# First layer's first gate vector summed on VectorE, with a chunk-by-chunk norm and a small-block scan

## The chip, the cores and the metric

One core of a Trainium2 chip runs the whole program. Its engines are named as in the profile: PE (TensorE matmuls) and PEld (its weight loads), DVE (VectorE), ACT (ScalarE), POOL (GpSimd) and SP (SyncE, which here only issues DMAs). The metric is the device time of one execution in microseconds, the median of several.

## The reference

Two layers of a hybrid network act on two groups of 128 tokens of width 2048: a prompt (group 0) and a sample (group 1). All is float32.

```
for l in 0, 1:
    shift1, scale1, gate1, shift2, scale2, gate2 = split(silu(c) @ w_mod[l] + b_mod[l], 6)   # one c a group
    h = x * (1 + scale1) + shift1
    q, k, v, hq, hff, hfb, hi, hgt = split(h @ w_in[l])            # 2048 -> 6656
    att = rms_norm(attention(q, k, v, sink))                       # 8 heads; sample also sees a cache
    hg  = rms_norm(scan_fwd + scan_bwd) * silu(hgt)                # 8 heads, chunks of 32 tokens
    x = layer_norm(ALPHA * x + gate1 * (concat(att, hg) @ w_o[l]))
    f = square(relu((x * (1 + scale2) + shift2) @ w_up[l])) @ w_down[l]   # 2048 -> 8192 -> 2048
    x = layer_norm(ALPHA * x + gate2 * f)
```

A scan, per head and chunk of 32 tokens: `o = tril(q e^b (k e^-b)^T) v + (q e^b) S` and `S = decay * S + (k e^(b_last - b))^T v`, with b the running sum of the log gates; the backward scan runs over the flipped tokens. The outputs are x of both groups, the prompt's k and v, and the prompt's final scan states.

## The kernel before

**Weights.** Every product with a weight matrix is done in tiles of 512 x 512. SP loads a tile as two halves of 128x1024 (`raw`, 10 buffers), ACT casts each half to fp32r (`wh`, line 1324) and DVE forms the rest (`wl = raw - wh`, line 1325); four `wh` and four `wl` buffers hold two tiles, and the split runs one tile ahead. The activations are split likewise, and PE adds three products, hi*hi, hi*lo, lo*hi (`mm_tile`, lines 436 to 450). A unit is the tiles that sum into one output, up to four of them (`groups`). Kind T (lines 436 to 439) leaves the output transposed, kind N (448 to 450) with tokens on partitions, one PSUM bank a token group. PSUM has three `acc` banks for the units, one for the modulation, four for the rest.

**Modulation.** A vector of 2048 of `c @ w_mod` reads 16 MB. `Mod` and `ModQ` multiply on PE with the two columns of c as weights (lines 203 and 223, four column groups at a time). `ModH` instead multiplies raw tiles by a scalar a partition and sums them in two accumulators on DVE (line 266; the first pass of a half on ACT, line 264), adds over the partitions with ones on PE (line 275) and stores a gate vector as a row in DRAM. `POOLED` lists the vectors done so; before, gate2 of layer 0 and shift1, scale1, gate1, gate2 of layer 1.

**Order.** `layer` writes one list `seq` of weight tiles, modulation items of 1 MB and calls. `RATE` says how many PE items follow a tile on the average, `PRATE` how many `ModH` items; `GAP` puts six PE items behind the first tile after a norm. Layer 0's in-projection runs over its 13 units three times (first 512 of the inputs, second, and the other half), since its modulation comes in quarters. Between tiles `pump` advances generators (attention, scans, norms) by a step each: up to two in the middle of a tile and up to three behind it, first come first. POOL and SP issue in the order of the program; the order on PE, DVE and ACT is chosen at compile time by the framework's scheduler. A tile name has a fixed number of buffers (`BUFS`: Y and Z 8, G, s0 and w 2).

**Scan** (`scan_task`). After the diagonal blocks (`pI`, line 748) the three later chunks get their products with all earlier ones, in three rounds, each with full 128-column weights (`pX`, line 777) and a scaling of the earlier keys before the next (line 774); a mask (`fx`, `bx`) copies the wanted blocks (line 794).

**Norm.** `ln_head` normalizes all eight pieces of 128x512 (line 909); then `ln_mod` goes chunk by chunk: transpose (931), scale and shift (group 0 on DVE in two passes, lines 934 and 936, group 1 on ACT, 940), split (408, 409). `ln_out` multiplies and adds the norm's own weights on POOL (1002, 1003) as soon as it is reached; after layer 0 its rows go to DRAM (1270).

Of the kernel before, what the change touches and what calls it, by code (L numbers as in the profile page):

```python
# [8 lines left out]
F32 = mybir.dt.float32  # L9
# [9 lines left out]
T = 128  # L19
# [42 lines left out]
def tile_hybrid_step(ctx: ExitStack, tc: tile.TileContext, a, o):  # L62
# [353 lines left out]
    def mm_tile(it, between):  # L416
# [6 lines left out]
        e = kg == un.groups[-1]  # L423
        for kk in range(2):
            if kk == 1:
                between()
            ks = range(2 * kk, 2 * kk + 2)
            if un.kind == "T":
                for m in range(4):
                    if f and kk == 0 and m % 2 == 0:  # L430
                        un.ps[m // 2] = accp.tile([128, 512], F32, tag="acc", name=nm("acc"))
                    ps = un.ps[m // 2][:, 256 * (m % 2):256 * (m % 2) + 256]
                    for k in ks:
                        w0 = wh[k][:, 128 * m:128 * m + 128]
                        w1 = wl[k][:, 128 * m:128 * m + 128]
                        pe.matmul(ps, lhsT=w0, rhs=hi[:, k], start=f and k == 0 and m % 2 == 0, stop=False,  # L436
                                  skip_group_check=True)
                        pe.matmul(ps, lhsT=w0, rhs=lo[:, k], start=False, stop=False, skip_group_check=True)  # L438
                        pe.matmul(ps, lhsT=w1, rhs=hi[:, k], start=False, stop=e and k == 3 and m % 2 == 1,  # L439
                                  skip_group_check=True)  # L440
            else:
                for g in range(2):
                    if f and kk == 0:
                        un.ps[g] = accp.tile([128, 512], F32, tag="acc", name=nm("acc"))
                    ps = un.ps[g]
                    gs = slice(128 * g, 128 * g + 128)
                    for k in ks:
                        pe.matmul(ps, lhsT=hi[:, k, gs], rhs=wh[k], start=f and k == 0, stop=False)  # L448
                        pe.matmul(ps, lhsT=hi[:, k, gs], rhs=wl[k], start=False, stop=False)  # L449
                        pe.matmul(ps, lhsT=lo[:, k, gs], rhs=wh[k], start=False, stop=e and k == 3)  # L450
# [233 lines left out]
    def scan_task(l, G, p, dr, z):  # L684
# [72 lines left out]
        mb = lambda s: masks[mk + s].unsqueeze(1).to_broadcast([128, 4, 128])  # L757
        dve.copy_predicated(v3(aT, 4), mb("i"), v3(pI, 4))
# [3 lines left out]
        order = [0, 1, 2, 3] if fwd else [3, 2, 1, 0]  # L762
        pX = bank("pX")
        qS = lf[:, 256:512]
        for i in range(1, 4):
            c = order[i]
            pc = order[:i]
            if i >= 2:
                sl = slice(min(pc[:-1]), max(pc[:-1]) + 1)
                n = i - 1  # L770
                d = dm[:, :, pc[-1]:pc[-1] + 1].unsqueeze(3).to_broadcast([128, 4, n, 32])
                kk = kdv[:, :, sl, :]
                flat = lambda x: x.rearrange("p m c t -> p m (c t)")
                dve.tensor_tensor(flat(kk), flat(kk),
                                  dm[:, :, pc[-1]:pc[-1] + 1].to_broadcast([128, 4, n * 32]), ALU.mult)
            for m in range(4):
                pe.matmul(pX[:, 128 * m + 32 * c:128 * m + 32 * c + 32], lhsT=kd[:, 128 * m:128 * m + 128],  # L777
                          rhs=qb[:, 128 * m + 32 * c:128 * m + 32 * c + 32], start=True, stop=True)
            if i == 1:
                cum = small(8).rearrange("p (h c) -> p h c", h=2)  # L780
                for hl in range(2):
                    m = 2 * hl + 1
                    dve.memset(cum[:, hl, order[0]:order[0] + 1], 1.0)
                    for x in range(1, 4):
                        pcol, ccol = order[x - 1], order[x]
                        dve.tensor_tensor(cum[:, hl, ccol:ccol + 1], cum[:, hl, pcol:pcol + 1],
                                          dm[:, m, pcol:pcol + 1], ALU.mult)
                for hl in range(2):
                    dve.tensor_tensor(
                        qS[:, 128 * hl:128 * hl + 128].rearrange("p (c t) -> p c t", c=4),  # L790
                        qbv[:, 2 * hl + 1], cum[:, hl, :].unsqueeze(2).to_broadcast([128, 4, 32]), ALU.mult)
            yield
        cs = slice(32 * min(order[1:]), 32 * max(order[1:]) + 32)
        dve.copy_predicated(v3(aT, 4)[:, :, cs],
                            masks[mk + "x"][:, cs].unsqueeze(1).to_broadcast([128, 4, 96]),
                            v3(pX, 4)[:, :, cs])
        pc = order[:3]
        lc = order[3]
        for m in (0, 2):
            sl = slice(128 * m + 32 * min(pc), 128 * m + 32 * max(pc) + 32)  # L800
            dve.tensor_scalar(kd[:, sl], kd[:, sl], dm[:, m, lc:lc + 1], None, ALU.mult)
# [67 lines left out]
    yt = {}  # L869
# [14 lines left out]
    def add_gated(key, n, g, ps, gt, first, last):  # L884
# [6 lines left out]
        else:  # L891
            (dve if n == 3 else pool).tensor_tensor(y, y, t, ALU.add)
# [10 lines left out]

    def ln_head(key):
        mr = ln_stat(key)
        for n in range(4):
            for g in range(2):
                y = yt[key, n, g]
                dve.tensor_scalar(y, y, mr[g][0], mr[g][1], ALU.subtract, ALU.mult)
# [11 lines left out]

    def ln_mod(key, AB, dst):

        A, B = AB
        for n in range(4):
            hl = new_act("h")
            for g in range(2):
# [5 lines left out]
                if g == 0:  # L933
                    dve.tensor_tensor(v3(t, 4), v3(pt, 4),
                                      A[:, 4 * n:4 * n + 4, g:g + 1].to_broadcast([128, 4, 128]), ALU.mult)
                    dve.tensor_tensor(v3(t, 4), v3(t, 4),
                                      B[:, 4 * n:4 * n + 4, g:g + 1].to_broadcast([128, 4, 128]), ALU.add)
                else:
                    for c in range(4):
                        act.activation(t[:, 128 * c:128 * c + 128], pt[:, 128 * c:128 * c + 128], AF.Identity,  # L940
                                       scale=A[:, 4 * n + c, g:g + 1], bias=B[:, 4 * n + c, g:g + 1])
# [51 lines left out]
    def ln_out(key, li, sink_fn):  # L993

        tag = "G"
# [488 lines left out]
```

## Time and profile before

| | |
|---|---|
| median of 3 runs | 2641.58 us (2641.39 to 2647.34) |
| profiled execution | 2641.68 us, span 2639.9 us |
| mean clock granted to TensorE | 0.988 |
| busy PE, PEld, DVE, ACT, POOL | 2536.6, 2178.1, 1862.5, 1214.5, 230.9 us |
| HBM | 643.32 MB read, 246 GB/s over the span |

Busy time is the union of an engine's instructions. A matmul's end is modelled, so PE counts as busy up to where the next one starts. The stages can be told by their lines: the first two rounds of layer 0 end near 122 and 222 us, its in-projection near 455, output projection near 608, MLP from 626 to 1391; then layer 1 with in-projection from 1409, output projection to 1880, MLP from 1898 to 2620, and the last norm.

### The profile page before, as it was taken

The numbers are of one execution on the slowest core, as the hardware profiler recorded it, in microseconds if no ns is written. First come the engines' busy times: TensorE is split into PE (matmuls) and PEld (weight loads), VectorE is DVE, ScalarE is ACT, GpSimd is POOL, SyncE is SP. The second block draws the span as 40 slices with busy tenths as digits, with TensorE's granted clock in tenths as the row PEclk, the third lists the DMA queues.
The fourth block names the chain that finished last, engine by engine and source line by source line (L and its number), as shares of the span: only waits on it lengthen the run. The fifth ranks groups of instructions, "written<-read, shape, count | busy, mean of one in ns | idle before, by whom it ended". The sixth has DMA issues, their size and how long they took to land.

```text
span 2639.9 us, 41114 instructions
## 1 busy us (share of the span) xinstructions
PE 2536.6 (96%) x16276; PEld 2178.1 (83%) x16276; DVE 1862.5 (71%) x2290; ACT 1214.5 (46%) x1655; POOL 230.9 (9%) x266
## 2 busy tenths in 40 slices
PE   7999999998999999999999999999799999999996
PEld 4787777756988979979887989888798998998985
DVE  3455777658887777887778888877865565656656
ACT  3434554434444533534434656644454454443442
POOL 2000000014100000000014100001420000000003
PEclk9999999999999999999999999999899999999998
DMA  9889778868887878787879556566566666666663
GB/s 359 287 283 324 265 244 273 297 231 323 281 307 276 276 261 287 265 281 258 287 251 331 195 191 204 177 228 212 186 225 208 222 202 227 212 207 225 205 206 115
DMA packets 192369, 652.91 MB, mean 247 GB/s; under 512 B 22752, under 2 KB 25376, under 8 KB 192176
## 3 DMA queue, kind: packets, MB, share of 16 engines
q1 hardware_dynamic: 177680, 614.56, 68.0%
q0 software_dynamic: 11552, 33.04, 4.4%
q8 instruction: 127, 2.08, 0.3%
q10 hardware_dynamic: 2944, 2.69, 0.3%
q14 instruction: 66, 0.54, 0.1%
HBM read 643.32 MB, written 6.88 MB: 246 GB/s over the span
## 4 chain that ended last, share of the span: by engine, by line
PE 76%; DMA 10%; DVE 9%; issue 3%; ACT 1%; SPq 0%; POOL 0%; DVEq 0%; ACTq 0%; POOLq 0%
PE acc L436 12%; PE acc L439 12%; PE acc L438 12%; PE acc L448 11%; PE acc L449 11%; PE acc L450 11%; DMA raw<-in_w_mod_dram 6%; DVE wl L1325 3%; DVE ma L266 2%; PE psm L203 2%; PE pX L777 1%; DMA raw<-in_w_up_dram 1%; DMA raw<-in_w_in_dram 1%; PE psm L223 1%; DMA out_nsf_dram<-lf 1%
## 5 line engine op out<-in xcount | busy, mean ns | idle before, releaser
L1324 ACT CAST wh<-raw 128x1024 fp32r<-128x1024 f32 x784 | 821.8, 1049 | 1140.3 <-PE acc L450 489.0
L1325 DVE TENSOR_TENSOR wl<-raw,wh 128x1024 fp32r<-128x1024 f32 x784 | 971.2, 1246 | 433.3 <-ACT wh L1324 406.6
L436 PE MATMUL acc<-hh,wh 128*128 128x256 f32 x3072 | 875.9, 285 | 3.4 <-DVE q L599 1.9
L439 PE MATMUL acc<-hh,wl 128*128 128x256 f32 x3072 | 870.5, 284 | 7.9 <-DVE wl L1325 7.7
L438 PE MATMUL acc<-hl,wh 128*128 128x256 f32 x3072 | 869.7, 283 | 1.2 <-DVE hl L409 1.2
L436 PEld LDWEIGHTS acc<-hh,wh 128*128 128x128 f32 x3072 | 589.0, 192 | 39.2 <-issue 26.0
L439 PEld LDWEIGHTS acc<-hh,wl 128*128 128x128 f32 x3072 | 588.6, 192 | 11.2 <-DVE wl L1325 10.4
L438 PEld LDWEIGHTS acc<-hl,wh 128*128 128x128 f32 x3072 | 589.0, 192 | 2.9 <-DVE hl L409 2.2
L266 DVE SCALAR_TENSOR_TENSOR ma<-raw,stat,ma 128x1024 f32<-128x1024 f32 x300 | 388.5, 1313 | 113.4 <-DMA raw<-in_w_mod_dram 111.8
L448 PE MATMUL acc<-wh,fh 128*128 128x512 f32 x1024 | 401.8, 392 | 7.0 <-DVE Z L1236 6.8
L449 PE MATMUL acc<-wl,fh 128*128 128x512 f32 x1024 | 400.4, 391 | 0.4 <-DVE wl L1325 0.4
L450 PE MATMUL acc<-wh,fl 128*128 128x512 f32 x1024 | 399.7, 390 | 0.0
L448 PEld LDWEIGHTS acc<-wh,fh 128*128 128x128 f32 x1024 | 193.0, 188 | 57.8 <-DVE Z L1236 8.1
L449 PEld LDWEIGHTS acc<-wl,fh 128*128 128x128 f32 x1024 | 193.0, 188 | 40.8 <-DVE wl L1325 1.5
L450 PEld LDWEIGHTS acc<-wh,fl 128*128 128x128 f32 x1024 | 193.1, 189 | 40.4
L448 PE MATMUL acc<-wh,hh 128*128 128x512 f32 x320 | 129.5, 406 | 3.0 <-ACT hh L408 2.4
L449 PE MATMUL acc<-wl,hh 128*128 128x512 f32 x320 | 127.5, 398 | 0.3 <-DVE wl L1325 0.3
L450 PE MATMUL acc<-wh,hl 128*128 128x512 f32 x320 | 125.9, 394 | 1.9 <-DVE hl L409 1.9
L448 PE MATMUL acc<-wh,mxh 128*128 128x512 f32 x256 | 105.0, 411 | 5.9 <-DVE G L887 5.3
L876 POOL DMA_DIRECT2D G<-gr x48 | 26.3, 548 | 953.2 <-DVE Z L1241 408.9
L203 PE MATMUL psm<-raw,stat 128*2 128x512 f32 x640 | 96.6, 598 | 8.1 <-DMA raw<-in_w_mod_dram 8.1
L450 PE MATMUL acc<-wh,mxl 128*128 128x512 f32 x256 | 101.5, 398 | 0.0
(366 smaller groups left out, 2124.6 us busy)
## 6 DMA issues: line engine op xcount, KB each, us to landing
raw<-in_w_mod_dram SPq DMA_DIRECT2D x384, 512.0 KB
raw<-in_w_up_dram SPq DMA_DIRECT2D x256, 512.0 KB
raw<-in_w_down_dram SPq DMA_DIRECT2D x256, 512.0 KB
raw<-in_w_in_dram SPq DMA_DIRECT2D x208, 512.0 KB
raw<-in_w_o_dram SPq DMA_DIRECT2D x64, 512.0 KB
G<-gr POOLq DMA_DIRECT2D x48, 256.0 KB, 5.1
G<-in_lng_dram POOLq DMA_DIRECT2D x12, 256.0 KB, 5.8
G<-in_lnb_dram POOLq DMA_DIRECT2D x12, 256.0 KB, 7.1
```

Of the source, the lines that this page charges most:

```text
L203: pe.matmul(self.ps[32 * j:32 * j + 2, :], lhsT=stat[:, k, :], rhs=raw[j // 2][:, 512 * (j % 2):512 * (j % 2) + 512], start=k == 0, stop=k ...
L223: pe.matmul(self.ps[32 * j:32 * j + 2, :], lhsT=stat[:, 4 * k + j, :], rhs=raw[j // 2][:, 512 * (j % 2):512 * (j % 2) + 512], start=k == 0 ...
L266: dve.scalar_tensor_tensor(self.acc[g], raw[h], c, self.acc[g], ALU.mult, ALU.add)
L436: pe.matmul(ps, lhsT=w0, rhs=hi[:, k], start=f and k == 0 and m % 2 == 0, stop=False, skip_group_check=True)
L438: pe.matmul(ps, lhsT=w0, rhs=lo[:, k], start=False, stop=False, skip_group_check=True)
L439: pe.matmul(ps, lhsT=w1, rhs=hi[:, k], start=False, stop=e and k == 3 and m % 2 == 1, skip_group_check=True)
L448: pe.matmul(ps, lhsT=hi[:, k, gs], rhs=wh[k], start=f and k == 0, stop=False)
L449: pe.matmul(ps, lhsT=hi[:, k, gs], rhs=wl[k], start=False, stop=False)
L450: pe.matmul(ps, lhsT=lo[:, k, gs], rhs=wh[k], start=False, stop=e and k == 3)
L777: pe.matmul(pX[:, 128 * m + 32 * c:128 * m + 32 * c + 32], lhsT=kd[:, 128 * m:128 * m + 128], rhs=qb[:, 128 * m + 32 * c:128 * m + 32 * c ...
L1324: act.copy(wh, r)
L1325: dve.tensor_tensor(wl, r, wh.bitcast(F32), ALU.subtract)
```

## The change

`gate1` of layer 0 joins `POOLED`, and its 16 items are placed by `PRATE` (0.3 an item in the second round, 0.5 in the third) while fewer PE items follow a tile there and in the output projection (`RATE` 0.8 for 1.2). The last tile of an N unit does group 0 whole, then group 1. The scan's cross blocks become two small products beside each other and a larger one, copied by ACT without masks, so two masks and their loads go. `ln_head` is merged into `ln_mod`, two pieces at a time; the scale and shift of group 0 is one pass a 128 columns. `ln_out` starts 24 steps later, goes six steps between a load and its use, and runs on DVE; so do the sums in `add_gated` and the product in `pre_sum`.

```diff
@@ derive_constants
-        for key in ("fi", "bi", "fx", "bx"):
+        for key in ("fi", "bi"):
@@ mm_tile
+        if un.kind == "N" and e:
+            for g in range(2):
+                if g == 1:
+                    between()
+                n_tile(un, g, range(4), hi, lo, wh, wl, f, e)
+            return
...
+    def n_tile(un, g, ks, hi, lo, wh, wl, f, e):
...
+        for k in ks:
+            pe.matmul(ps, lhsT=hi[:, k, gs], rhs=wh[k], start=f and k == 0, stop=False)
+            pe.matmul(ps, lhsT=hi[:, k, gs], rhs=wl[k], start=False, stop=False)
+            pe.matmul(ps, lhsT=lo[:, k, gs], rhs=wh[k], start=False, stop=e and k == 3)
@@ scan_task
-        for i in range(1, 4):
...
-            for m in range(4):
-                pe.matmul(pX[:, 128 * m + 32 * c:128 * m + 32 * c + 32], lhsT=kd[:, 128 * m:128 * m + 128],
-                          rhs=qb[:, 128 * m + 32 * c:128 * m + 32 * c + 32], start=True, stop=True)
...
+        def across(ss, ts):
+            for m in range(4):
+                pe.matmul(pX[rows(ss), cols(m, ts)], lhsT=kd[:, cols(m, ss)], rhs=qb[:, cols(m, ts)],
+                          start=True, stop=True, tile_position=(0, 32 * ss.start))
+        across(one(c0), one(c1))
+        across(one(c2), one(c3))
...
+        dve.tensor_tensor(kdv[:, :, c0], kdv[:, :, c0], dm[:, :, c1:c1 + 1].to_broadcast([128, 4, 32]), ALU.mult)
+        dve.tensor_tensor(qbv[:, :, c3], qbv[:, :, c3], dm[:, :, c2:c2 + 1].to_broadcast([128, 4, 32]), ALU.mult)
+        across(early, late)
+        yield
+        for ss, ts in ((one(c0), one(c1)), (one(c2), one(c3)), (early, late)):
+            act.copy(aTv[rows(ss), :, rows(ts)], v3(pX, 4)[rows(ss), :, rows(ts)])
@@ add_gated
-            (dve if n == 3 else pool).tensor_tensor(y, y, t, ALU.add)
+            dve.tensor_tensor(y, y, t, ALU.add)
@@ scale_shift, ln_mod
+        for c in range(4):
+            o_, s_ = (x[:, 128 * c:128 * c + 128] for x in (out, src))
+            if g == 0:
+                dve.tensor_scalar(o_, s_, A[:, c, g:g + 1], B[:, c, g:g + 1], ALU.mult, ALU.add)
+            else:
+                act.activation(o_, s_, AF.Identity, scale=A[:, c, g:g + 1], bias=B[:, c, g:g + 1])
...
+        mr = ln_stat(key)
         for n in range(4):
+            for g in (1, 0):
+                y = yt[key, n, g]
+                dve.tensor_scalar(y, y, mr[g][0], mr[g][1], ALU.subtract, ALU.mult)
+            for g in (1, 0):
...
+                scale_shift(t, pt, A[:, fs], B[:, fs], g)
@@ ln_out
+        for _ in range(24):
+            yield
         for n in range(4):
...
+            for _ in range(6):
+                yield
             for g in range(2):
-                pool.tensor_tensor(y, y, gt, ALU.mult)
-                pool.tensor_tensor(y, y, bt, ALU.add)
+                dve.tensor_tensor(y, y, gt, ALU.mult)
+                dve.tensor_tensor(y, y, bt, ALU.add)
                 sink_fn(n, g, y)
-            yield
+                for _ in range(3):
+                    yield
-    POOLED = ((0, 5), (1, 0), (1, 1), (1, 2), (1, 5))
+    POOLED = ((0, 2), (0, 5), (1, 0), (1, 1), (1, 2), (1, 5))
-    PRATE = {(0, "r1"): 0, (0, "r2"): 0, (0, "in"): 0, (0, "o"): 0, ...
+    PRATE = {(0, "r1"): 0, (0, "r2"): 0.3, (0, "in"): 0.5, (0, "o"): 0, ...
@@ pre_sum
-                    pool.tensor_tensor(t, t, gch[l, 5, n, g, 0], ALU.mult)
+                    dve.tensor_tensor(t, t, gch[l, 5, n, g, 0], ALU.mult)
-    RATE = {(0, "in"): 1.2, (0, "o"): 1.2, (0, "mlp"): 0.111, ...
+    RATE = {(0, "in"): 0.8, (0, "o"): 0.8, (0, "mlp"): 0.111, ...
```

## Rows read from the trace of the kernel before

**Rows 1.** Chain that ended last, shares of the span by engine, whole run.

```profile
PE 76%; DMA 10%; DVE 9%; issue 3%; ACT 1%; SPq 0%; POOL 0%; DVEq 0%; ACTq 0%; POOLq 0%
```

**Rows 2.** Stretches: length, busy PE, PEld, DVE, ACT, POOL (instructions), PE clock, DMA share, GB/s.

```profile
122.00:222.00 100.00, 99.11 (x679) 76.91 (x679) 56.25 (x72) 35.33 (x43) 0.00 (x0) 0.98 0.85 299
222.00:455.00 233.00, 223.71 (x1599) 180.23 (x1597) 167.06 (x326) 118.69 (x198) 10.57 (x20) 0.99 0.80 274
455.00:608.00 153.00, 145.42 (x736) 99.22 (x733) 95.98 (x175) 56.53 (x119) 20.13 (x26) 0.99 0.78 263
608.00:626.00 18.00, 14.48 (x89) 4.74 (x88) 15.09 (x28) 4.24 (x11) 7.99 (x8) 1.00 1.03 409
626.00:1391.00 765.00, 750.73 (x4789) 663.39 (x4790) 612.73 (x564) 349.51 (x395) 46.85 (x40) 1.00 0.81 276
1898.00:2620.00 722.00, 718.58 (x4616) 656.00 (x4614) 443.31 (x399) 328.81 (x370) 47.01 (x48) 1.00 0.63 206
```

**Rows 3.** Timeline of PE, 440 to 444 us: start, length, line, tiles, shape, count.

```profile
440.51 0.98 PE L777 MATMUL pX<-ed,t 128*128 128x32 f32 x8
441.42 1.90 PE L203 MATMUL psm<-raw,stat 128*2 128x512 f32 x16
443.25 0.39 PE L436 MATMUL acc<-hh,wh 128*128 128x256 f32 x1
443.47 0.28 PE L438 MATMUL acc<-hl,wh 128*128 128x256 f32 x1
443.59 0.28 PE L439 MATMUL acc<-hh,wl 128*128 128x256 f32 x1
```

**Rows 4.** Line 203 alone in two stretches: length, busy PE, PEld, clock, DMA.

```profile
222.00:455.00 233.00, 33.04 (x248) 3.89 (x248) 0.99 0.80 274
455.00:608.00 153.00, 25.94 (x148) 2.87 (x144) 0.99 0.78 263
```

**Rows 5.** Groups of DVE by line: count, busy us, mean ns, idle before, releasers.

```profile
L266 DVE SCALAR_TENSOR_TENSOR ma<-raw,stat,ma 128x1024 f32<-128x1024 f32 x300 | 388.5, 1313 | 113.4 <-DMA raw<-in_w_mod_dram 111.8 <-ACT ma L264 1.2
L801 DVE TENSOR_SCALAR ed<-ed,s 128x96 f32<-128x96 f32 x16 | 3.7, 263 | 2.9 <-PE pX L777 2.9
```

**Rows 6.** Groups of weight loads (PEld) by line.

```profile
L777 PEld LDWEIGHTS pX<-t,ed 128*128 128x128 f32 x192 | 23.6, 192 | 0.6
L203 PEld LDWEIGHTS psm<-raw,stat 128*2 128x2 f32 x640 | 11.2, 82 | 42.4 <-issue 20.0 <-DMA raw<-in_w_mod_dram 18.3 <-DVE w L279 0.4
```

**Rows 7.** Timeline of all engines at the third boundary, 1880 to 1899 us.

```profile
1886.25 6.60 DVE L909 TENSOR_SCALAR Y<-Y,s,s 128x512 f32<-128x512 f32 x8
1888.92 1.51 ACT L940 ACTIVATE ed<-pt,B,A 128x128 f32<-128x128 f32 x4 [3.50 <-PE pt L931]
1892.77 1.28 DVE L934 TENSOR_TENSOR ed<-pt,A 128x512 f32<-128x512 f32 x2
1895.97 0.75 PE L436 MATMUL acc<-hh,wh 128*128 128x256 f32 x2
```

**Rows 8.** Line 909 on its own: count, ns min/median/max, first and last start.

```profile
L909 DVE TENSOR_SCALAR Y<-Y,s,s x16: 540/543/1503, 613.1 to 1891.4; 128x512 f32<-128x512 f32 x16
```

**Rows 9.** Timeline of PE at the first boundary.

```profile
617.19 1.03 PE L203 MATMUL psm<-raw,stat 128*2 128x512 f32 x4 [0.92 <-DMA raw<-in_w_mod_dram]
```

**Rows 10.** Waits of PE: who waited for whom, us in total, times, longest.

```profile
PE acc L448 <- DVE Z L1236: 6.8, 3, 2.4
PE acc L448 <- DVE G L887: 5.3, 2, 3.5
```

**Rows 11.** Timeline of POOL, ACT and DVE in layer 1's in-projection, 1455 to 1492 us.

```profile
1460.06 0.58 POOL L1270 DMA_DIRECT2D xscr<-Z  x1 [0.30 <-POOL Z L1003]
1477.98 0.59 ACT L456 COPY Z<-acc 128x512 f32<-128x512 f32 x1 [0.56 <-PE acc L439]
1489.45 0.68 DVE L752 TENSOR_TENSOR ed<-ed,Z 128x512 f32<-128x512 f32 x1
```

**Rows 12.** The chain that ended last, 28 to 42 us: start, length, what.

```profile
32.50 5.06 DMA mbi<-in_mbi_dram
```

More of the change, by code (lines that the diff above doesn't have):

```diff
@@ new lines, in mm_tile @@
+            if un.kind == "N":
+                for g in range(2):
+                    n_tile(un, g, ks, hi, lo, wh, wl, f, e)
+                continue
+            for m in range(4):
+                if f and kk == 0 and m % 2 == 0:
+                    un.ps[m // 2] = accp.tile([128, 512], F32, tag="acc", name=nm("acc"))
+                ps = un.ps[m // 2][:, 256 * (m % 2):256 * (m % 2) + 256]
+                for k in ks:
+                    w0 = wh[k][:, 128 * m:128 * m + 128]
+                    w1 = wl[k][:, 128 * m:128 * m + 128]
+                    pe.matmul(ps, lhsT=w0, rhs=hi[:, k], start=f and k == 0 and m % 2 == 0, stop=False,
+                              skip_group_check=True)
+                    pe.matmul(ps, lhsT=w0, rhs=lo[:, k], start=False, stop=False, skip_group_check=True)
+                    pe.matmul(ps, lhsT=w1, rhs=hi[:, k], start=False, stop=e and k == 3 and m % 2 == 1,
+                              skip_group_check=True)
@@ new lines, in n_tile @@
+    def n_tile(un, g, ks, hi, lo, wh, wl, f, e):
+        if f and ks[0] == 0:
+            un.ps[g] = accp.tile([128, 512], F32, tag="acc", name=nm("acc"))
+        ps = un.ps[g]
+        gs = slice(128 * g, 128 * g + 128)
+        for k in ks:
+            pe.matmul(ps, lhsT=hi[:, k, gs], rhs=wh[k], start=f and k == 0, stop=False)
+            pe.matmul(ps, lhsT=hi[:, k, gs], rhs=wl[k], start=False, stop=False)
+            pe.matmul(ps, lhsT=lo[:, k, gs], rhs=wh[k], start=False, stop=e and k == 3)
@@ L793, in scan_task @@
[L793 to L801, printed above, removed]
+        c0, c1, c2, c3 = order = [0, 1, 2, 3] if fwd else [3, 2, 1, 0]
@@ new lines, in scan_task @@
+        early, late = slice(min(c0, c1), max(c0, c1) + 1), slice(min(c2, c3), max(c2, c3) + 1)
+        cols = lambda m, sl: slice(128 * m + 32 * sl.start, 128 * m + 32 * sl.stop)
+        rows = lambda sl: slice(32 * sl.start, 32 * sl.stop)
+        one = lambda c: slice(c, c + 1)
+        pX = bank("pX")
+        def across(ss, ts):
+            for m in range(4):
+                pe.matmul(pX[rows(ss), cols(m, ts)], lhsT=kd[:, cols(m, ss)], rhs=qb[:, cols(m, ts)],
+                          start=True, stop=True, tile_position=(0, 32 * ss.start))
@@ new lines, in scan_task @@
+        across(one(c0), one(c1))
+        across(one(c2), one(c3))
+        qS = lf[:, 256:512]
+        cum = small(8).rearrange("p (h c) -> p h c", h=2)
+        do = dm[:, 1::2]
+        dve.memset(cum[:, :, c0:c0 + 1], 1.0)
+        for x in range(1, 4):
+            pc, cc = order[x - 1], order[x]
+            dve.tensor_tensor(cum[:, :, cc:cc + 1], cum[:, :, pc:pc + 1], do[:, :, pc:pc + 1], ALU.mult)
+        for hl in range(2):
+            dve.tensor_tensor(qS[:, 128 * hl:128 * hl + 128].rearrange("p (c t) -> p c t", c=4),
+                              qbv[:, 2 * hl + 1], cum[:, hl, :].unsqueeze(2).to_broadcast([128, 4, 32]), ALU.mult)
@@ new lines, in scan_task @@
+        yield
[3 more added lines that the diff above has]
+        yield
+        aTv = v3(aT, 4)
+        for ss, ts in ((one(c0), one(c1)), (one(c2), one(c3)), (early, late)):
+            act.copy(aTv[rows(ss), :, rows(ts)], v3(pX, 4)[rows(ss), :, rows(ts)])
+        de = small(2).unsqueeze(2)
@@ L802, in scan_task @@
+        dg = dm[:, 0::2]
+        kg = kdv[:, 0::2]
+        dve.tensor_tensor(de, dg[:, :, c2:c2 + 1], dg[:, :, c3:c3 + 1], ALU.mult)
+        flat = lambda x: x.rearrange("p m c t -> p m (c t)")
+        dve.tensor_tensor(flat(kg[:, :, early]), flat(kg[:, :, early]), de.to_broadcast([128, 2, 64]), ALU.mult)
+        dve.tensor_tensor(kg[:, :, c2], kg[:, :, c2], dg[:, :, c3:c3 + 1].to_broadcast([128, 2, 32]), ALU.mult)
         yield
@@ L920, in ln_coef, with scale_shift @@
         return A, B
+    def scale_shift(out, src, A, B, g):
+        for c in range(4):
[4 more added lines that the diff above has]
+                act.activation(o_, s_, AF.Identity, scale=A[:, c, g:g + 1], bias=B[:, c, g:g + 1])
     def ln_mod(key, AB, dst):
         A, B = AB
+        mr = ln_stat(key)
         for n in range(4):
             hl = new_act("h")
-            for g in range(2):
+            fs = slice(4 * n, 4 * n + 4)
+            for g in (1, 0):
+                y = yt[key, n, g]
+                dve.tensor_scalar(y, y, mr[g][0], mr[g][1], ALU.subtract, ALU.mult)
+            for g in (1, 0):
                 y = yt[key, n, g]
@@ L1068, in first_h @@
             x = xT[n][g]
[L1069 to L1075 removed]
+            scale_shift(x, x, s1, sh, g)
             split_act(hl, (slice(None), slice(0, 4), slice(128 * g, 128 * g + 128)), v3(x, 4))
```

84 lines of the change are left out of this document (5 added, 79 removed).

## The prediction

> **What bounds the kernel now.** I read the chain of waits first: PE holds 76% of it, DMA 10%, DVE 9% [rows 1]. Then the stages, one stretch each [rows 2]. The last one, the second layer's MLP, has 128 weight tiles in 722.0 us, 5.64 us a tile, with PE busy 718.6: that is what a tile costs when nothing disturbs it. Layer 0's MLP needs 765.0 us for the same 128 tiles, and DVE is busy 612.7 of them. Layer 0's in-projection (its second half of the weights, 26 tiles, from 222 us on) takes 233.0 us with PE busy 223.7 and DVE 167.1; the output projection 153.0 with PE busy 145.4. The reader is to see that PE bounds nearly all of it, so a PE instruction taken out is worth its time unless another engine is late in its place. The exceptions are the boundaries between an output projection or MLP and the next stage, some 18 us each: in the first one DMA is at 1.03 of its engines.
>
> The profiled execution took 2641.7 us (span 2639.9 and 1.8 around it), the median of the three timed ones is 2641.58. The sum goes from 2641.7.
>
> **The gate vector, on PE.** 16 items, each two groups of four instructions, leave PE (line 203). Two items run from 441.42 to 443.25, 0.92 us each, and the first matmul behind them is followed after 0.22 us, where the next ones follow after 0.12 [rows 3]. I take 0.95 us an item. In the in-projection 26 tiles took 1.2 items each, 31 (the 248 instructions of the view, 8 an item [rows 4]); at 0.8 they take 21: -10 us. The small-block scan adds -3 (below), so PE goes from 223.7 to 211, and with the 9 us that it stood idle the stage would be 220.
>
> **The gate vector, on DVE.** The steps of 0.3 and 0.5 a tile put 3 items of it into the second round (13 tiles) and 13 into the 26 tiles. An item is 3.75 passes over 128x1024 (60 over 16 items; the first of each half runs on ACT) of 1.295 us, busy 388.5 over 300 [rows 5]: 4.9 us, 63 us for 13. The scan gives back 1.3 us (estimated: a masked copy, two scalings of 0.263 [rows 5] and three products go, some shorter ones come) for each of the 7 scans in the stretch, 9 in all. So DVE goes from 167.1 to 221 of 233. On top, these passes waited 111.8 us for their weights in the whole run [rows 5], which is 1.4 us an item, 18 for 13, during which nothing behind them on DVE moves, the splits of the next weights (line 1325) first. That makes 221 to 239 on DVE against 220 on PE. The ends: -13 us if DVE keeps up, +12 if it sets the pace with some idle of its own. The nearest row is layer 0's MLP, where DVE's 612.7 and most of those waits stand beside PE busy 98% of the time [rows 2]: DVE that full cost PE little. I take -3, that is 230 us.
>
> The second round gets 3 more items of 1 MB beside its 29. Its DMA share of 0.85 becomes 0.94; the first boundary has run at 1.03 [rows 2]. 0 to +5, I take +2.
>
> **Output projection of layer 0.** 16 tiles at 1.2 items become 0.8: 19 to 13 items. Here an item costs more, 25.94 us for 18.5 of them, 1.4 [rows 4], since they come in pieces that wait for DMA: -8.4 for 6. Some of them only fill gaps that attention leaves on PE. -9 to 0, I take -7. The last gate item now comes at the 25th of the 26 tiles, and its sum, its store to DRAM and the load of the gates follow. Cover: the last scans, for which the first tiles of the output projection wait anyway, and two tiles until the first eviction. Were the cover gone, a store and a load like the 5.06 us of [rows 12], 10 us. Six additions that POOL did come to DVE, which is busy 96 of 153 [rows 2].
>
> **Small-block scan.** Per scan 24 instructions stay 24, with weights of 32 or 64 columns for 128, in two groups for three. A group of eight lasts 0.91 us (440.51 to 441.42 [rows 3]), so 2.7 a scan. A weight load of 128 columns is 192 ns, one of two columns 82 [rows 6]: if the pace goes with it, 1.2 is the lower end. The upper end is the old pace and four hand-overs of 0.1 us (the 0.22 against 0.12 above): 3.1. I take 2.3, -0.4 a scan: -3 for the second layer's eight scans; those of the first are in the stage above. Ends for the eight: -12 and +3.
> A rule speaks against this term. The rows show 0.1 us lost behind the column groups of line 203 [rows 3]. The Trainium skill, TensorEngine Tiling (Array Packing), Key Properties, says that a change of the tiling mode, not of the tile alone, drains the engine. By an estimate from that rule, with the 0.28 us that a matmul lasts in [rows 3] for a drain, the 64 changes of 16 scans would cost 18 us, 12 more than at 0.1, and the sum would end near 2628; that is inside the forecast's own range. No row here shows a 64-column step directly behind a 32-column one.
>
> **Chunk-by-chunk norm.** Third boundary [rows 7]: the statistics are done at 1886.25, eight norms take 6.60 us, the scale and shift of the first chunk wait behind them until 1892.77, the first matmul starts at 1895.97, 9.7 us after the statistics. Now two norms (1.1) come first, the transposes follow (0.6), then ACT's 1.51 and two casts (0.6 each, estimated from the norm's 0.54): some 4 us. POOL's passes, beside which a norm took up to 1503 ns for a median of 543 [rows 8], are off the place. Four short scalings a chunk are 4 x 0.263 at most [rows 5] for two passes of 0.64. -5.8 there. In the first boundary PE runs modulation items at the pace of DMA until 618, each four instructions after 0.92 us of waiting for their weights [rows 9], and the next weights are late too: -2. The second has the same six items: -3. Together -11; ends -4 and -18.
>
> **Order of the last N tile.** The first of two accumulators is now complete half a tile (2.7 us) before the end, not a quarter. PE waited 6.8 and 5.3 us for evictions [rows 10]; its weight loads stood for the same events. -5, ends -12 and 0. The price would be weights: the second half is needed at a quarter of the tile, not at a half; they are split a tile ahead, 5.6 us, which covers the 1.4 us. Were that cover gone, 1.4 us for each of the 68 such tiles, 95 us. At the end of the kernel one half's 2 us of evictions go below matmuls that hid only part: -0.7.
>
> **POOL's work to DVE.** 48 passes with the norms' weights, 12 adds, 16 products, 0.64 us each (two in 1.28 [rows 7]): 49 us of DVE, 15 of them in each of the two MLPs. Cover: DVE is busy 443.3 of 722.0 in one and 612.7 of 765.0 in the other [rows 2], and gets back there what POOL slowed. Zero. Were the cover gone, 15 us in layer 0's.
>
> **Delayed ln_out.** Before layer 1 all eight Z buffers hold its rows. The weights' loads now come 24 steps later, two steps a tile: at the 12th tile, where the first gate unit must be evicted into two Z. Before, the last row was stored at 1460.06 and that eviction was at 1477.98 [rows 11]. Now the first row goes at the 15th tile in POOL's order, the second behind the state loads of the next scans, which wait for a late step of the first ones. A Z is read out 11.5 us after its eviction (1489.45 [rows 11]); two in series, 23 us, meet the 23 us of the next unit's four tiles. 0 to +20, I take +2.
>
> **Masks.** A 5.06 us load of the second mask is on the chain at 32.50 [rows 12]; two of four loads go. -0.5.
>
> **Sum.** -0.5 + 2 - 3 - 7 - 11 - 5 - 0.7 - 3 + 2 = -26.2; 2641.7 becomes 2615.5 us.
>
> **Rivals.**
> *Fillers.* The items on PE sat in gaps, and the first two boundaries are DMA's: then the output projection gives 0, the boundaries -3, the in-projection +4 and the sum is -4: 2637.5. For it: PE waits in pieces for line 203's weights [rows 9]. Against: PE is busy 96% of the in-projection [rows 2].
> *VectorE becomes the bound (the slower side).* Place: layer 0's in-projection, from the first gate of the scans on. Its price is 63 + 18 - 9 = 72 us of DVE time against the 66 us that DVE stood idle (233.0 less 167.1 [rows 2]). If half is absorbed the stage grows by 36 instead of shrinking by 3: 2641.7 - 26.2 + 39 = 2654.5. It decides for slower once less than 41 of the 72 are absorbed. For it: DVE's idle there is waiting for other engines, which does not move at will. Against: the MLP above.
> *Held Z buffers.* The +20 instead of +2: 2633.5. For it: the counts above. Against: a scheduler that places DVE's passes early, as soon as the loads are in.
> *More than that.* The good ends of the five large terms, -13 -9 -18 -12 -12, with the small ones -1.2: about 2576. That the change doesn't do what it says shows at once if line 203 still has 640 instructions; I give it nothing.
>
> **Chances.** Forecast (2600 to 2630) 0.58, larger gain 0.08, fillers 0.14, held Z 0.10, VectorE 0.10. A measurement here tells 0.3% (8 us) from none: faster is below 2633.7. Half of held Z and a little of the fillers fall there: faster 0.74, same 0.16, slower 0.10. The range leaves out the far ends of the larger gain and of VectorE: 2584 to 2648; the likeliest case's own is 2600 to 2630.
>
> **What would show it.** Line 203 with 512 instructions for 640, and line 266 with 360 passes for 300. The in-projection near 230 us with DVE above 90%: PE waiting there often for the split weights would prove the VectorE rival. First matmul some 4 us after the statistics at the third boundary. ACT's eviction of the first gate unit of layer 1 waiting for the store of a Z would show held Z. The prediction is wrong if the in-projection is above 245 us, or if stretches other than the in-projection, the output projection and the boundaries move by more than 10.

## The result and the profile after

The changed kernel takes 2624.08 us (median of 4, 2620.16 to 2628.0) where the kernel before takes 2641.48: a ratio of 0.9929, 95% interval 0.9909 to 0.9949, so 0.7% faster. The forecast was 2615.5. The profiled execution has 2620.16, its span 2618.4: 21.5 less than before, where the sum had 26.2. Direction and size look nearly right; the experiments show that they are right for the wrong reasons, by luck.

First the page of the changed kernel (busy time and share of each engine, instructions; chain by engine) and its groups of the two lines that carry the gate vector.

```profile
PE 2517.6 (96%) x16164; PEld 2157.3 (82%) x16164; DVE 1917.1 (73%) x2393; ACT 1232.6 (47%) x1706; POOL 105.1 (4%) x188
PE 78%; DVE 10%; DMA 7%; issue 2%; ACT 2%; SPq 0%; ACTq 0%; DVEq 0%
L266 DVE SCALAR_TENSOR_TENSOR ma<-raw,stat,ma 128x1024 f32<-128x1024 f32 x360 | 454.2, 1281 | 112.6 <-DMA raw<-in_w_mod_dram 110.4
L203 PE MATMUL psm<-raw,stat 128*2 128x512 f32 x512 | 86.8, 596 | 9.5 <-DMA raw<-in_w_mod_dram 7.4
```

Line 203 has its 512 instructions and line 266 its 360 passes: the change does what it says. Now the stretches of the changed kernel (columns as in [rows 2]): second round, layer 0's in-projection, its output projection, first boundary, layer 0's MLP. The length of a stretch less PE's busy time is called PE's idle time below.

```profile
125.80:224.90 99.10, 98.04 (x668) 75.33 (x669) 62.70 (x79) 34.88 (x43) 0.00 (x0) 0.98 0.90 319
225.00:461.80 236.80, 220.49 (x1542) 174.24 (x1544) 217.28 (x341) 129.81 (x226) 6.46 (x12) 0.96 0.77 275
461.80:616.90 155.10, 141.19 (x678) 96.94 (x677) 105.47 (x192) 57.70 (x120) 14.81 (x28) 0.96 0.71 244
616.90:631.00 14.10, 11.77 (x79) 3.80 (x78) 10.39 (x28) 5.02 (x14) 3.01 (x6) 1.00 0.97 359
631.00:1388.50 757.50, 748.93 (x4800) 662.95 (x4798) 615.48 (x598) 347.01 (x390) 12.62 (x24) 1.00 0.82 281
```

Cut at its own events in the same way (the scale and shift of the second and of the last quarter of the activations, the last in-projection and the last output-projection matmul), the kernel before has the first three so; its in-projection is 5 us shorter here than in [rows 2], whose cuts were round numbers:

```profile
123.10:221.80 98.70, 98.08 (x670) 76.01 (x671) 55.66 (x69) 35.10 (x42) 0.00 (x0) 0.98 0.85 299
222.00:450.10 228.10, 220.97 (x1583) 178.69 (x1581) 162.16 (x311) 113.80 (x191) 10.57 (x20) 0.99 0.80 275
450.00:608.50 158.50, 148.76 (x752) 100.96 (x750) 101.45 (x192) 61.53 (x126) 20.13 (x26) 0.98 0.78 262
```

The second round is 0.4 us longer (forecast 2), but starts 2.7 later. The in-projection is 8.7 longer where 3 less was forecast; the output projection 3.4 shorter (forecast 7). The three boundaries, from the start of a stage's last matmul to the start of the next stage's first, are 2.1, 2.6 and 4.1 shorter (forecast 2, 3 and 5.8). Between these matmuls layer 0's MLP is 9.3 shorter and layer 1's in-projection 6.9, where the forecast had little or nothing. PE waits in layer 0's in-projection for what is on VectorE (PE's waits there in the changed kernel: us in total, times, longest):

```profile
PE acc L448 <- DVE wl L1329: 4.6, 4, 2.7
PE acc L457 <- DVE pa L469: 4.2, 1, 4.2
PE pX L780 <- DVE t L797: 3.2, 2, 2.1
PE acc L458 <- DVE wl L1329: 1.9, 2, 0.9
```

Line 1329 splits the weights, line 469 evicts an accumulator, line 797 is the scan's. In the kernel before PE waits there for no weight split, and for nothing longer than 2.4 us. The granted clock counts too. Busy PE times the clock is, roughly (the clock has two digits), PE's work in us at the full 2.4 GHz: 220.97 x 0.99 = 218.8 before and 220.49 x 0.96 = 211.7 now, so 7.1 were saved. Idle went from 7.1 to 16.3, and what the clock took from 2.2 to 8.8: 15.8 lost, 8.7 net.

### The profile page after: what moved, and what is told of

Same layout as the page of the kernel before. It is cut to its first block, busy times and chain, and to the rows that moved or that the text cites. A ratio compares the mean times of both kernels' runs of the same rounds, so it can differ in the third digit from the quotient of the medians.

```text
span 2618.4 us, 41018 instructions
## 1 busy us (share of the span) xinstructions
PE 2517.6 (96%) x16164; PEld 2157.3 (82%) x16164; DVE 1917.1 (73%) x2393; ACT 1232.6 (47%) x1706; POOL 105.1 (4%) x188
## 4 chain that ended last, share of the span: by engine, by line
PE 78%; DVE 10%; DMA 7%; issue 2%; ACT 2%; SPq 0%; ACTq 0%; DVEq 0%
PE acc L445 13%; PE acc L448 13%; PE acc L447 13%; PE acc L457 11%; PE acc L458 11%; PE acc L459 11%; DMA raw<-in_w_mod_dram 5%; DVE wl L1329 3%; DVE ma L266 2%; PE psm L203 2%; DMA raw<-in_w_in_dram 1%; PE psm L223 1%; ACT wh L1328 1%; PE pX L780 1%; PE pt L947 1%
## 5 line engine op out<-in xcount | busy, mean ns | idle before, releaser
L1329 DVE TENSOR_TENSOR wl<-raw,wh 128x1024 fp32r<-128x1024 f32 x784 | 950.8, 1222 | 361.8 <-ACT wh L1328 345.3
L266 DVE SCALAR_TENSOR_TENSOR ma<-raw,stat,ma 128x1024 f32<-128x1024 f32 x360 | 454.2, 1281 | 112.6 <-DMA raw<-in_w_mod_dram 110.4
L458 PE MATMUL acc<-wl,mxh 128*128 128x512 f32 x256 | 100.9, 395 | 1.6 <-DVE wl L1329 1.6
L203 PE MATMUL psm<-raw,stat 128*2 128x512 f32 x512 | 86.8, 596 | 9.5 <-DMA raw<-in_w_mod_dram 7.4
```

The lines of the kernel that those rows point to most:

```text
L203: pe.matmul(self.ps[32 * j:32 * j + 2, :], lhsT=stat[:, k, :], rhs=raw[j // 2][:, 512 * (j % 2):512 * (j % 2) + 512], start=k == 0, stop=k ...
L266: dve.scalar_tensor_tensor(self.acc[g], raw[h], c, self.acc[g], ALU.mult, ALU.add)
L1329: dve.tensor_tensor(wl, r, wh.bitcast(F32), ALU.subtract)
```

## Experiments

Ratios are against the kernel before, run beside each on the same chip; "us" is the ratio times 2641.5. The changed kernel's own 0.9929 is -19 us so. Experiments 1 to 5 ask what the gate vector's move costs and how; 6 to 12 run the other parts one by one. The stretches come from one profiled execution of each kernel, the ratios from all of its executions.

**1. The gate vector back on PE.** All else of the change stays.

```diff
-    POOLED = ((0, 2), (0, 5), (1, 0), (1, 1), (1, 2), (1, 5))
+    POOLED = ((0, 5), (1, 0), (1, 1), (1, 2), (1, 5))
-    PRATE = {... (0, "r2"): 0.3, (0, "in"): 0.5, ...}   RATE = {(0, "in"): 0.8, (0, "o"): 0.8, ...}
+    PRATE = {... (0, "r2"): 0, (0, "in"): 0, ...}   RATE = {(0, "in"): 1.2, (0, "o"): 1.2, ...}
```

> The changed kernel with the gate vector (0, 2) back on PE, the three rates as before; everything else of the change stays. Theory 1: the move of the gate vector is a loss, since VectorE (217 of 236.8 us busy in layer 0's in-projection) makes PE wait more than the removed instructions free; the stage goes back to about 225 us (228.1 of before less the scan's 3), the second round to 100, the output projection to about 157, and the kernel to about 2612 us, 10 to 12 under the changed one. Theory 2 (the one of the forecast): the move is a gain and something else lengthened the stage, the new scan or the order of the last N tile; then the stage stays above 235 us and the kernel goes to about 2634, 10 above the changed one.

Measured: 2595.77 us, ratio 0.9807 (0.9790 to 0.9824), -51 us. Theory 1, and by far more than it asked: this beats both kernels. Its place is only half right: the in-projection goes back by 6.4 us, the output projection, which was to stay near 157, by 18.9. Its in-projection and output projection:

```profile
225.00:455.40 230.40, 220.95 (x1632) 171.71 (x1631) 168.86 (x316) 128.33 (x236) 10.58 (x20) 0.99 0.79 274
455.40:591.60 136.20, 135.42 (x705) 93.55 (x703) 93.76 (x165) 52.95 (x105) 11.27 (x21) 1.00 0.87 304
```

With 19 items on PE in the output projection, PE is busy 135.4 of 136.2 us at the full clock; with 12 (the changed kernel) 141.2 of 155.1 at 0.96. That fits items that had filled gaps; experiment 5 has 12 items beside as much other work. The two stages must be read as a sum, 366.6 here and 391.9 there, since attention's work moves between them (553 PE instructions besides the items here, 584 there).

**2. The move alone**, on the kernel before; the edit above, reversed.

> The kernel before with only the gate vector (0, 2) moved to VectorE, with the three rates of the change. Theory 1 (the move is a loss): in-projection of layer 0 at 238 us or more (228.1 before), second round 103, output projection 153 to 156; the kernel at 2645 to 2655 us, against 2641.5. Theory 2 (the move is a gain): in-projection at or under 226, the kernel at 2628 to 2634. If both sizes cancel: 2641, and the gain of the change is all in its other parts.

Measured: 2678.46 us, ratio 1.0121 (1.0105 to 1.0138), +32 us, above theory 1's upper end. In-projection 249.5 us (DVE 219.0, clock 0.94), output projection 156.1. On the kernel before it costs what it costs on top of the rest (0.9929 over 0.9807 is 1.24%). PE waits 15.0 us for weight splits in this in-projection, once for 7.7.

**3. Half of the passes.**

```diff
-                    else:
+                    elif (self.l, self.v) != (0, 2) or g == 0:
                         dve.scalar_tensor_tensor(self.acc[g], raw[h], c, self.acc[g], ALU.mult, ALU.add)
```

> The changed kernel with half of VectorE's passes for the gate vector (0, 2) left out (one of the two batch rows keeps its first product alone, so that part of the gates is not computed); loads, order of the items and waits for the loads stay. Theory 1a (the passes' busy time makes PE wait): 32 us of VectorE time go, some 26 of them in layer 0's in-projection, the stage falls from 236.8 to about 226 and the kernel from 2624 to about 2612. Theory 1b (what costs is that passes wait for their weights and hold the splits queued behind them): the stage stays within 3 us of 236.8 and the kernel within 4 of 2624.

Measured: 2605.33 us, ratio 0.9842 (0.9822 to 0.9862), 23 us under the changed kernel. The in-projection and the output projection:

```profile
224.60:441.80 217.20, 210.29 (x1537) 167.88 (x1536) 189.49 (x318) 129.35 (x227) 6.48 (x12) 1.00 0.84 299
441.80:593.30 151.50, 139.57 (x681) 95.80 (x679) 102.78 (x190) 57.06 (x119) 14.87 (x28) 0.97 0.75 250
```

Together 368.7, nearly as with the vector on PE (366.6). PE's work is 210, close to the 211.7 of the changed kernel, idle 6.9, and the clock takes nothing. With all the loads still made, leaving out half of VectorE's passes gives back 23 of the 25 us that these two stages lost and 23 of the kernel's 32. 1b falls.

**4. Earlier items**, 0.6 a tile for 0.3 in the second round.

> The changed kernel with the gate vector's items placed earlier: 0.6 a tile instead of 0.3 in the second round, so that 8 of 16 lie there and the last comes at tile 16 of 26 of layer 0's in-projection. VectorE's time in the in-projection falls by 5 items, about 25 us, as in the kernel with half the passes, but no pass is left out. Theory 1a (VectorE's busy time): the in-projection falls from 237 to 218 to 222 us, the second round grows by 4 to 6 for five more loads and passes, and the kernel is 2605 to 2612. Rival 'late row' for layer 0's output projection, which took 155 us with the items on VectorE, 151.5 with half the passes and 136 with the items on PE: if the gate row that comes at the 25th tile is what holds it, it falls to 136 to 142 here and the kernel to about 2595; if not, it stays at 150 or more.

Measured: 2645.54 us, ratio 0.9992 (0.9978 to 1.0006): 17 us slower than the changed kernel, against theory 1a. The premise failed: five items of the next vector moved up into the in-projection, which keeps 218 us of VectorE and takes 257.1. The second round takes 110.1 for 99.1: three items were free there, five more cost 11 us. The output projection is 140.6, as 'late row' asked, but with the in-projection it makes 397.7: no gain.

**5. Earlier items, no others behind them.**

```diff
-                if poolseq:
+                if poolseq and (prate not in (0.5, 0.6) or (poolseq[0][0].l, poolseq[0][0].v) == (0, 2)):
```

> The changed kernel with 0.6 items a tile in the second round, as in the run before, and no other vector's items behind them: there five items of the next vector followed into layer 0's in-projection, so that VectorE had as much to do in it (219 us) as in the changed kernel and only the row came earlier. Here eight items lie in the in-projection and VectorE has some 25 us less. Theory 1a (VectorE's busy time sets this stage): 218 to 224 us for 241 there, as with half the passes; second round 108 to 112, as in the run before; layer 0's output projection 140, the row being early; the kernel 2600 to 2608. Rival 'place': the early items delay the second round and the tiles behind it, and what follows is late whatever VectorE has to do; then the in-projection stays above 235 and the kernel above 2620.

Measured: 2632.99 us, ratio 0.9951 (0.9931 to 0.9971). 'Place', against theory 1a. Second round, in-projection and output projection:

```profile
127.00:234.70 107.70, 98.60 (x666) 75.23 (x666) 79.71 (x97) 31.73 (x40) 1.95 (x5) 0.97 0.91 329
234.70:488.00 253.30, 228.75 (x1570) 181.29 (x1569) 210.32 (x349) 134.14 (x238) 9.77 (x19) 0.93 0.73 252
488.00:623.80 135.80, 129.84 (x650) 93.44 (x648) 94.74 (x166) 54.82 (x108) 10.73 (x20) 1.00 0.76 260
```

VectorE is busy 83% of a stage that is 16 us longer than with 92%. So its total busy time alone doesn't set the stage. PE's waits for the weight splits (line 1329) do tell these kernels apart: 12.1 us here, against 6.5 in the changed kernel and 1.5 with half of the passes. In experiment 1 and the kernel before PE waits for none. First this kernel, then experiment 3:

```profile
PE acc L448 <- DVE wl L1329: 7.6, 2, 5.0
PE acc L458 <- DVE wl L1329: 4.5, 3, 2.9
```

```profile
PE acc L458 <- DVE wl L1329: 0.9, 1, 0.9
PE acc L448 <- DVE wl L1329: 0.6, 2, 0.3
```

The longest of these waits shows what the split is late behind. From this kernel's timelines, first VectorE (start, length, line), then the matmul of PE that waits:

```profile
367.11 1.28 DVE L266 SCALAR_TENSOR_TENSOR ma<-raw,stat,ma 128x1024 f32<-128x1024 f32 x1
368.31 0.49 DVE L793 TENSOR_TENSOR lf<-ed,s 128x128 f32<-128x128 f32 x2
368.71 2.47 DVE L266 SCALAR_TENSOR_TENSOR ma<-raw,stat,ma 128x1024 f32<-128x1024 f32 x2
371.11 2.35 DVE L1329 TENSOR_TENSOR wl<-raw,wh 128x1024 fp32r<-128x1024 f32 x2
```

```profile
372.38 0.58 PE L448 MATMUL acc<-hh,wl 128*128 128x256 f32 x1 [4.98 <-DVE wl L1329]
```

Three gate passes, 3.7 us, stand ahead of the split that PE stands still for, 4.98 us (367.4 to 372.4). In the slice from 370 to 380, which holds the end of this wait, the granted clock is 0.66. PE's work is 228.75 x 0.93 = 213, as in the others; 24.6 us idle and some 16 of the clock make the rest. The place of the passes in VectorE's queue is shown for this wait; that it explains the others is inferred. Why more such waits come together here than in the changed kernel, which has five items more in the stage, no run tells; PE waited 5.1 us for loads of modulation weights too.

**6. Order of the last N tile alone** (the two functions of the diff, on the kernel before).

> The kernel before with only the order of the last N tile changed. All of the change but the gate vector gave 1.9% (50 us), against some 18 in the forecast's terms, so at least one term was far too small. The forecast's term for this one is -5.7 (waits of 6.8 and 5.3 us for evictions, less the tail): 2636 for a before of 2641.5. Rival theory 'order': an accumulator that is ready half a tile earlier also frees VectorE and ScalarE to split the weights in time in layer 0's output projection, whose every second tile is such a one; then layer 0's output projection shrinks by 10 or more from 158.4 us and the kernel by 15 to 25. Rival 'sum': the parts help one another and each alone gives no more than its term.

Measured: 2625.30 us, ratio 0.9917 (0.9902 to 0.9931), -22 us: 'order'. Layer 0's output projection:

```profile
447.70:595.80 148.10, 143.69 (x751) 100.07 (x750) 98.80 (x184) 59.77 (x124) 21.04 (x26) 0.99 0.82 277
```

10.4 us less; idle PE falls from 9.7 to 4.4, and the same 152 instructions of line 203 are busy 23.7 us where they were 27.0. Layer 0's MLP gains 6, layer 1's output projection 4. The places and sizes are those of 'order'; that the splits come earlier, its reason, is not shown.

**7. Small-block scan alone**, with its masks.

> The kernel before with only the small-block scan and its two masks less. The forecast's terms for it: -0.4 us a scan, 16 scans, and -0.5 for the masks, -7 in all: 2634.5. Rival 'scan': what counts is not TensorE's time but VectorE's masked copy over 384 columns and one round of waiting less, which lets the splits through in layer 0's in-projection and in the scans of its output projection; then these two stages shrink by 15 or more together and the kernel by 20. Rival 'drain' (the Trainium skill, TensorEngine Tiling (Array Packing), Key Properties): the mode changes cost, and the kernel gains nothing or loses up to 5.

Measured: 2634.51 us, ratio 0.9939 (0.9923 to 0.9956), -16 us: between the terms and 'scan'; 'drain' falls. In the changed kernel's timeline of PE:

```profile
337.96 0.40 PE L457 MATMUL acc<-wh,hh 128*128 128x512 f32 x1
338.20 0.39 PE L458 MATMUL acc<-wl,hh 128*128 128x512 f32 x1
338.51 0.59 PE L780 MATMUL pX<-ed,t 128*32 128x32 f32 x16
339.03 0.50 PE L459 MATMUL acc<-wh,hl 128*128 128x512 f32 x1
339.37 0.40 PE L457 MATMUL acc<-wh,hh 128*128 128x512 f32 x1
477.08 0.68 PE L780 MATMUL pX<-ed,t 128*64 128x64 f32 x8
477.69 0.50 PE L459 MATMUL acc<-wh,mxl 128*128 128x512 f32 x1
```

An old group of eight in the kernel before, with the matmuls around it:

```profile
446.22 0.98 PE L777 MATMUL pX<-ed,t 128*128 128x32 f32 x8
447.03 0.36 PE L436 MATMUL acc<-hh,wh 128*128 128x256 f32 x1
447.23 0.28 PE L438 MATMUL acc<-hl,wh 128*128 128x256 f32 x1
```

Sixteen 32-column steps take 0.52 us to the next matmul, eight 64-column ones 0.61, 1.13 in all. An old group takes 0.81 (the 0.91 of [rows 3] stands in front of line 203), three of them 2.43. The full-width matmuls follow one another after 0.24; into the small steps it is 0.31, and behind the first matmul after them 0.34. But the old group, which changes no mode, also loses 0.1 behind it: 0.20 where 0.12 is the pace [rows 3]. So a change of mode costs some 0.1 us on the way in and no more than an old group on the way out. Counted with all of these, a scan takes some 1.5 us for 2.7, and 16 scans save some 19; the kernel gained 16. The rule of the Trainium skill (TensorEngine Tiling (Array Packing), Key Properties) that a change of mode drains the engine may hold, but its price here is 0.1 us and no drained 0.28 us matmul. Whether the small steps are fast for their narrow weights or for standing beside each other in the array, no run separates.

**8. Chunk-by-chunk norm alone** (ln_mod, scale_shift, first_h of the diff, on the kernel before).

> The kernel before with only the chunk-by-chunk norm and the scale and shift by single chunks. The forecast's term is -11: third boundary 16.0 to 10.2 us, first -2, second -3; 2630 for a before of 2641.5. ScalarE-bound rival: the third boundary gains under 3 and the kernel under 5. Rival 'norm': the norms' 64 VectorE passes beside the stage's other work were the cost, and the kernel gains 20 or more.

Measured: 2648.90 us, ratio 1.0008 (0.9997 to 1.0020): nothing, outside all three expectations. The third boundary does shrink, from 16.2 to 12.2 us. But behind the second one its first 40 us read so (the kernel before, then this one):

```profile
1391.00:1411.00 20.00, 14.66 (x93) 6.50 (x92) 17.65 (x30) 7.40 (x17) 9.41 (x10) 1.00 1.01 386
1411.00:1431.00 20.00, 20.00 (x95) 16.68 (x94) 19.99 (x18) 13.04 (x21) 10.00 (x8) 1.00 0.80 280
```

```profile
1393.70:1413.70 20.00, 17.03 (x97) 8.62 (x96) 15.84 (x34) 8.22 (x20) 9.11 (x10) 0.91 1.00 378
1413.70:1433.70 20.00, 15.32 (x56) 12.07 (x55) 19.64 (x22) 9.38 (x14) 9.13 (x8) 0.83 0.69 233
```

PE gains 2.4 us in the first 20 and loses 4.7 in the next, waiting for splits, and the clock falls to 0.83: here the early start is given back. The scale and shift of the second quarter starts at 125.65 where it was 123.07; in all runs with the old form it starts by 123.2, in all with the new one at 125.4 or later.

**9. Old norm in the version of experiment 1.**

> The changed kernel with the gate vector back on PE (0.9807 of before) and with the old norm too, all eight norms ahead of the first scale and shift, the scale and shift of one row in two wide passes. The chunk-by-chunk norm alone, on the kernel before, gave 1.0008. Theory 'with the delay': its gain shows only where the output rows of the norm are no longer computed in the same stretch, as here; then this kernel is 8 to 11 us slower than with the new norm, 0.984 to 0.985 of before. Rival: the early start is given back in the next tiles either way; then the ratio stays within 0.979 to 0.982.

Measured: 2596.18 us, ratio 0.9812 (0.9786 to 0.9838): the rival. The delay of the output rows does not make the norm pay either.

**10. GpSimd's passes and the delay together** (add_gated, pre_sum, ln_out of the diff, on the kernel before).

> The kernel before with only GpSimd's passes of the norms' weights, the gated adds and the pre-sum moved to VectorE, and the layer norm's output rows delayed by 24 steps. The forecast's terms: 0 and +2, 2643.5. Rival 'contention': GpSimd's passes slowed VectorE (norms up to 1503 ns for a median of 543), so that the stretches behind the boundaries gain 5 to 10 and the kernel 10. Rival 'held Z': +10 to +20 at the start of layer 1.

Measured: 2628.60 us, ratio 0.9926 (0.9908 to 0.9944), -20 us: the size of 'contention' twice over, its places only in part: layer 0's MLP is 5.7 us shorter, layer 1's in-projection 3.5 longer. One group of GpSimd in the kernel before, then the same passes on VectorE in the changed one:

```profile
L1002 POOL TENSOR_TENSOR Y<-Y,G 128x512 f32<-128x512 f32 x16 | 30.7, 1920 | 35.8 <-DMA G<-in_lng_dram 20.3 <-PE pt L931 12.6 <-DVE ed L934 2.9
```

```profile
L1013 DVE TENSOR_TENSOR Y<-Y,G 128x512 f32<-128x512 f32 x16 | 10.7, 689 | 7.9 <-DMA G<-in_lng_dram 7.9
```

The whole page of this run has VectorE busy 1857.6 us with 76 passes more than the kernel before, which has 1862.5: what came over, some 50 us, VectorE got back on its other passes (the splits fell from 1246 to 1222 ns, the gate passes from 1313 to 1281, 28 us in these two). So passes on GpSimd do slow VectorE's.

**11. The adds and the pre-sum alone.**

```diff
-            (dve if n == 3 else pool).tensor_tensor(y, y, t, ALU.add)
+            dve.tensor_tensor(y, y, t, ALU.add)
```

> The kernel before with only the gated adds and the pre-sum moved from GpSimd to VectorE. With the output rows moved and delayed as well it gave 0.9926 (-19 us). Theory 'adds': they sit between the eviction of an accumulator and what is next, and a GpSimd pass beside VectorE is slow; then this kernel alone has 12 to 19 us of it, with layer 0's output projection and layer 1's each 4 to 5 shorter and the third boundary 3: 0.993 to 0.9955. Rival 'output rows': the 48 passes of the norm's weights just behind the first two boundaries are what cost; then this one is 0.998 to 1.001.

Measured: 2639.56 us, ratio 0.9976 (0.9959 to 0.9994), -6 us: a third of experiment 10, between both theories. The output projections are 3.0 and 4.4 us shorter, near what 'adds' asked; the third boundary is not.

**12. The delay alone**, the rows' passes left on GpSimd (ln_out of the diff with pool for dve).

> The kernel before with only the layer norm's output rows delayed by 24 steps, their passes left on GpSimd. Theory 'adds': 0.998 to 1.001, the stretches behind the boundaries moving by no more than 3. Rival 'output rows, their place': 0.993 to 0.996, the first 40 us behind the second boundary with PE at 20 of 20 and norm passes at their undisturbed 0.54 us. Rival 'held Z': 1.002 to 1.008, layer 1's in-projection longer by 5 to 20.

Measured: 2650.32 us, ratio 1.0025 (1.0008 to 1.0042), +7 us: the low end of 'held Z', though no run shows that Z is what it waits for. Layer 1's in-projection is 10.2 us longer, but it is 9.6 and 6.6 longer in experiments 8 and 11 too, which delay nothing. By difference, 0.9926 over 0.9976 and 1.0025 is 0.9925: if the parts add up, some 20 us are the rows' passes going from GpSimd to VectorE.

## Why the prediction was right in sum and wrong in its terms

Alone, the parts give +32 (gate), -22 (order), -16 (scan), -20 (GpSimd and delay), +2 (norm): -24, near the -19 of the whole. The forecast had about -5, -6, -7, +2 and -11. Four are outside their own ends: the gate (its three ends add up to +17 at most), the order (-12), the norm (-4) and GpSimd's passes, which were to give nothing. The errors cancel, so the total came out by luck. The signs of being wrong that the prediction named stayed away (the in-projection is at 236.8 of 245, and layer 0's MLP moved by 9.3 of 10): lengths of whole stages don't show errors that cancel.

- *The gate vector* failed at the step "DVE that full cost PE little", taken from layer 0's MLP. VectorE is busy 80% there [rows 2], 92% here, and here PE waited for it in pieces. The other end, +12, was nearer, and the rival *VectorE becomes the bound* names the place and, with PE's waits for the splits, the mechanism; by its size it would have decided if the other parts had been as small as forecast. The PE side was right: the stage would be 220 "if DVE keeps up", and was 217.2 in experiment 3.
- *Output projection, -7*: the rival *Fillers* was right in its sign. Seven items fewer gave nothing (136.2 us with 19 items and 553 other PE instructions, 135.8 with 12 and 554 in experiment 5). The late gate row, costed at nothing under the last scans, does stand in the chain of the changed kernel (start, length, what):

```profile
484.66 0.25 ACTq L294
485.32 4.35 DMA gr<-w
489.69 1.29 ACT w L857 x8
```

  Its store holds the buffer that ACT, at line 857 in the norm of the scans' output, waits 5.9 us for. How much of the 155 us is due to it is open: where the row was early, attention's work had moved too.
- *Second round, +2*: 0.4; 98.7 to 99.1.
- *Norm, -11*: the step itself was right (from the end of the statistics, 1871.00, to the first matmul, 1876.70, 5.7 us, where 9.7 was and 4 was forecast; the forecast's own steps add up to 4.4). That a boundary made shorter makes the kernel shorter was wrong.
- *Scan, 2.3 us of 1.2 to 3.1*: some 1.5 with the changes of mode, near the lower end. The weight load's median does fall, from 192 ns [rows 6] to 113. The term of -0.4 a scan was a third of the -1.2 it should have been.
- *Masks, -0.5*: the load in [rows 12] is `mbi`, which stays. In experiment 7, without the other two masks, it is still on the chain with 5.03 us. That term had no ground.
- *Order, -5*: the waits of [rows 10] are only those that PE's records name. In layer 0's output projection an eviction is 1.8 us of the 9.7 that PE idled; the others are loads of modulation weights (3.1), the scan (2.2) and attention (1.9). With the order alone these shrink too; why they do is not shown.
- *POOL's work, 0*: 0.64 us a pass was VectorE's price; on GpSimd the passes took 1.35 to 1.92 us, by the means of their groups, and what they had slowed on VectorE weighed as much as they do there. "Gets back there what POOL slowed" was the right step, and its gain was not counted.
- *Held Z, +2*: the delay alone costs +7 with the passes on GpSimd, inside 0 to +20; its reason stays open.

## What to carry over

Count a term where the stage ends, not where the wait is seen: an early start at a boundary came to nothing, and filler work taken from TensorE did too. An engine that feeds TensorE can cost time before it is full, when long passes stand ahead of the feeding ones in its queue: 4.98 us of waiting behind three gate passes, in a stage with VectorE at 83%. Such gaps can be paid again in the granted clock (0.93 in that stage), though not all are: the output projection behind it idled 6.0 us at 1.00. When a change of several parts lands near the forecast, run each part alone: here one part lost 32 us while others gained 58, and the change without it is the fastest version, 1.9% under the kernel before, with the new norm or the old.

## What was not expected of the hardware

Of the 15.8 us that layer 0's in-projection lost, 6.6 are the clock: the clock went from 0.99 to 0.96. In experiment 5 the 10 us that hold the end of the 4.98 us wait have 0.66 of 2.4 GHz, so the greater part of them is at 1.2, while the stage with the items on PE keeps 0.99 (experiment 1). One group of GpSimd's 128x512 products beside VectorE took 1920 ns each for VectorE's 689. A matrix step with a 32-column weight and 32 moving columns costs 33 ns (0.52 us for 16), one with 64 and 64 costs 76, one with 128 and 32 costs 101 (0.81 for 8).
